# A hybrid decoder layer: v and gate products as a pinned three-step pipeline, norms by one-column sums and a way through DRAM, rotations swapped by ScalarE, merges with six open products

## The chip, the cores and the metric

The kernel runs on one core of one Trainium2 chip. The metric is the device time of one execution in microseconds. The kernel before takes 2696.99 us, the median of 3 runs (2695.11 to 2697.38).

## The reference

One layer of a decoder trunk over 512 tokens with 2048 channels (D), everything in float32. From the normalized and modulated u a combined projection gives the columns of three token mixers, their SiLU gates z and three merge gates g:

```python
u = rms_norm(x, norm_w) * (1.0 + scale) + shift        # shift, scale, gate from silu(c) @ w_ada + b_ada
proj = einsum('bsd,de->bse', u, w_in)                  # 2048 x 23552
o_a = diff_attention(a_q, a_k, a_v)    # 8 heads, two softmaxes of width 64, rms_norm over the head's 128
o_b = retention(b_q, b_k, b_v)         # 8 heads of 64, rotated q and k, decay, rms_norm over the head's 128
o_c = dilated_mixture(c_q, c_k, c_v)   # 3 groups x 8 heads, windows with dilation 1, 4, 16
y_a = (o_a * silu(a_z)) @ w_proj_a     # likewise y_b and y_c: 1024 x 2048
merged = sigmoid(g_a) * y_a + sigmoid(g_b) * y_b + sigmoid(g_c) * y_c
out = rms_norm(x + gate * (merged @ w_out), final_norm_w)
```

`rms_norm(o)` is `o * rsqrt(mean(o*o) + 1e-6) * w`. The rotation of a pair (2i, 2i+1) in a head of B is `x * cos + rot * sin`, where rot swaps the two numbers of the pair and turns the sign of one.

## The kernel before, in words

**Precision.** Every large product is made of three float32r products. `mm3` (L151-154) takes the rounded operands (h) and what the rounding left (l) and adds h·h, h·l and l·h into one PSUM tile. So each weight tile is first split: ScalarE copies the loaded tile r to h, VectorE subtracts, l = r − h. Activations lie transposed: channels on partitions, the 512 tokens along the free axis (`uh`, `ul`, 16 tiles of 128x512). PSUM has two tiles named `pj` and six named `at`, each 128x512. Weights pass through `wr`, `wh`, `wl` with three buffers each (L124-128).

**Stages.** After the start (norm, modulation, u, and the columns of the C gate, nine of its sixteen tiles without the shift's part) come in this order:

- The *units* (L488-665). Nine products of u with 1024 columns of `w_in`, each by seven products of half-size blocks instead of eight (in Winograd's way): three groups of v for C, one of v for A, one for B, and four half gates of A and B. A unit is a list of jobs: P1, P2 and R3 with two steps each (a step is four row tiles of 128 by 512 columns, one load of 1 MB into `xr`), then eight steps in which `sum_prep` adds blocks of the weights (four additions, L583) and `sum_mul` feeds four products R6, R5, R7 and Q4. Each step splits its tile, `xh` by ScalarE (L552, L584) and `xl` by VectorE (L553, L585); `xr` has three buffers, `xh` and `xl` two. The token forms fh, fl (sums of blocks of u) are built by `form_build` in the first eight steps from u read back out of DRAM. When P1, P2, R3 or the sums are complete, `keep`, `p2_done` or `sum_done` combine them; `put` writes the result to DRAM, for gate units after a sigmoid on ScalarE (L636). Job i + 1 is prepared ahead of the products of job i (L655-661). The order of the units' early halves is set by hand (L646): the plain steps of unit 3, then those of unit 2.
- The *C heads* (eight passes): per head seven projections (`proj`, L156-170: 2048 channels by 128 columns, 48 products) with scores, softmax and values of the head before placed at the middle of a projection (`mid`). Each pass starts with `bias_step` (L810-816): GpSimd computes, for one of nine 128-column tiles of the C gate, what the shift adds (`gate_bias_load`, L674-687, four loads, `br` with one buffer); one pass later TensorE sums it over the partitions (`gate_bias_sum`, L689-692).
- The *C merge*: `gate_phase` (L695-742) with mode "first". For each of sixteen tiles of 128 output channels: eight mm3 over the mixer's channels (yh, yl), times the sigmoid of the gate, plus the partial sum of the mixers before. `gate_cols` loads the gate's tile into `gsg` (two buffers), the partial sum comes back through `gpr` (one buffer) and goes out to `part_dram`. Three tiles are started ahead with six of their eight mm3 (`y_start`), and after each of them one piece of the last head's remaining work (`left`) is placed; the rest are started and closed one by one. `aux` adds a part of the output gate (product of c with `w_ada`, L756-796) behind each tile.
- The *A heads* (L1046-1087): q, k, scores, softmax (`a_scores`), transposes (`a_turn`), values, then the norm: `rms_squares` (L979-988) squares the output in halves, adds the halves, splits the sum into h and l on 64 partitions each; `rms_gate` (L990-998) sums over the partitions and spreads the sum with one 128x512 product with ones, takes root and reciprocal of the whole 128x512 tile, multiplies by the weight, the norm and silu(z), and `put_y` splits the result into yh and yl. The pieces of head n stand in the middle of the projections of head n + 1.
- The *A merge* ("mid"), the *B heads* in four pairs (L1128-1169; `rotate`, L1099-1107, with q and k of two heads side by side; even and odd numbers of the pairs lie in separate groups of 32 partitions, so the swap is a shift by 32 partitions), and the *B merge* ("last"), whose sums mh, ml stay in SBUF for the last product with `w_out`.

**What sets the order.** Each engine runs its instructions in one order. The framework's planner sets it at build time: it plays the program with costs of its own and takes the first instruction, in the order of the program, that its model says is ready. `tc.keep_in_program_order(instr)`, which the kernel before doesn't use in the functions below, holds an instruction behind the one traced before it on the same engine. DMAs are issued in each issuing engine's order: loads of weights, gates and partial sums by SyncE (SP), partial sums out by ScalarE, units' results and broadcasts by GpSimd.

## Time and profile before

| | |
|---|---|
| median of 3 runs | 2696.99 us (2695.11 to 2697.38) |
| the profiled execution's own time | 2694.27 us |
| its span in the profile | 2692.5 us |
| TensorE (PE) busy | 2578.1 us, 96% |
| VectorE (DVE) busy | 1695.3 us, 63% |
| ScalarE (ACT) busy | 1034.6 us, 38% |
| GpSimd (POOL) busy | 268.9 us, 10% |
| HBM read and written | 405.56 and 40.44 MB |

The profile is one execution. Times are microseconds from the span's start. PE stands for TensorE's products, PEld for its weight loads, which overlap them; SPq, ACTq and POOLq are the queues through which these engines issue DMAs. L552 is line 552 of the kernel before. A row "PE at L152 <- ACT yh L218: 11.8, 3, 6.4" says that PE, ahead of line 152, waited 11.8 us in total for ScalarE's writing of yh in line 218, three times, 6.4 us at the longest. PEclk is the granted clock of TensorE, 1.00 being full. By stage the span divides at about 239 (units begin), 964 (C heads), 1662 (C merge), 1756 (A heads), 2066 (A merge), 2184 (B heads), 2414 (B merge) and 2520 us (last product).

### The profile page before, as it was taken

Reading aid. Unit: us, or ns where it says so; the run is one execution under the profiler, and the core shown is the slowest. Engines: PE = TensorE matmul, PEld = TensorE weight load, DVE = VectorE, ACT = ScalarE, POOL = GpSimd, SP = SyncE. Lnnn points to the kernel's source line nnn. Section 1 sums busy time; section 2 is a strip of 40 time slices with the busy share of each in tenths; the row PEclk is TensorE's granted clock in tenths of the full one; section 3 lists DMA queues with packets and bytes.
Section 4 is the critical chain, followed back from the end, with each engine's and each line's share of the span. In section 5 each row is a group of like instructions: output and inputs, shape, how many; then the busy total and the mean of one; then the engine's idle time right before and its main releaser. Section 6 shows DMA issues by size and latency. Waiting matters only on the chain.

```text
span 2692.5 us, 33258 instructions
## 1 busy us (share of the span) xinstructions
PE 2578.1 (96%) x13091; PEld 2188.5 (81%) x13091; DVE 1695.3 (63%) x2456; ACT 1034.6 (38%) x1388; POOL 268.9 (10%) x271
## 2 busy tenths in 40 slices
PE   6899999999999999899999999999999899998998
PEld 5677878789999988788888888788887677777888
DVE  7995887877787744334443444657766667776434
ACT  4234433333343433333333333246665134443222
POOL 3432000000000022132211220000000000000000
PEclk9999999999999999999999999999999899999999
DMA  9776666666656655334444444943232773325632
GB/s 347 247 275 239 231 212 219 219 220 209 212 196 204 208 145 137 94 106 126 113 118 108 112 125 128 286 126 87 86 94 84 231 236 90 106 82 176 219 102 102
DMA packets 413420, 448.17 MB, mean 166 GB/s; under 512 B 24696, under 2 KB 308042, under 8 KB 412112
## 3 DMA queue, kind: packets, MB, share of 16 engines
q1 hardware_dynamic: 383784, 395.61, 46.6%
q0 software_dynamic: 9760, 33.59, 4.0%
q10 hardware_dynamic: 19720, 16.86, 1.8%
q8 instruction: 102, 1.67, 0.3%
q14 instruction: 54, 0.44, 0.1%
HBM read 405.56 MB, written 40.44 MB: 166 GB/s over the span
## 4 chain that ended last, share of the span: by engine, by line
PE 78%; DVE 12%; DMA 5%; ACT 2%; issue 2%; POOL 0%; SPq 0%; DVEq 0%; ACTq 0%; POOLq 0%
PE pj L154 15%; PE pj L153 15%; PE pj L152 15%; PE at L154 10%; PE at L153 10%; PE at L152 10%; DVE acc L312 3%; DMA xr<-in_w_in_dram 2%; DVE xl L553 1%; DMA part<-gsg 1%; DVE rt L1105 1%; DVE rs L995 1%; DMA gpr<-part 1%; DVE wl L148 1%; ACT xh L552 1%
## 5 line engine op out<-in xcount | busy, mean ns | idle before, releaser
L154 PE MATMUL pj<-uh,wl 128*128 128x512 f32 x1552 | 610.2, 393 | 12.1 <-DVE wl L148 9.5
L152 PE MATMUL pj<-uh,wh 128*128 128x512 f32 x1552 | 614.1, 396 | 4.8 <-ACT wh L147 4.8
L153 PE MATMUL pj<-ul,wh 128*128 128x512 f32 x1552 | 608.5, 392 | 0.0
L148 DVE TENSOR_TENSOR wl<-wr,wh 128x1024 fp32r<-128x1024 f32 x226 | 282.4, 1251 | 368.0 <-ACT wh L147 349.2
L147 ACT CAST wh<-wr 128x1024 fp32r<-128x1024 f32 x228 | 239.0, 1050 | 540.3 <-PE pj L153 395.3
L154 PEld LDWEIGHTS pj<-uh,wl 128*128 128x128 f32 x1552 | 293.8, 189 | 76.3 <-DVE wl L148 11.9
L152 PEld LDWEIGHTS pj<-uh,wh 128*128 128x128 f32 x1552 | 294.1, 189 | 63.9 <-ACT wh L147 5.0
L153 PEld LDWEIGHTS pj<-ul,wh 128*128 128x128 f32 x1552 | 294.0, 189 | 58.6
L584 ACT CAST xh<-xr 128x2048 fp32r<-128x2048 f32 x72 | 137.6, 1912 | 235.8 <-PE at L154 104.1
L583 DVE TENSOR_TENSOR xr<-xr 128x512 f32<-128x512 f32 x288 | 197.3, 690 | 41.5 <-DMA xr<-in_w_in_dram 36.0
L585 DVE TENSOR_TENSOR xl<-xr,xh 128x2048 fp32r<-128x2048 f32 x72 | 164.7, 2289 | 43.3 <-ACT xh L584 43.1
L152 PE MATMUL at<-yh,wh 128*128 128x512 f32 x384 | 155.2, 405 | 18.4 <-ACT yh L218 11.8
L553 DVE TENSOR_TENSOR xl<-xr,xh 128x2048 fp32r<-128x2048 f32 x54 | 123.8, 2293 | 55.3 <-ACT xh L552 54.8
L154 PE MATMUL at<-yh,wl 128*128 128x512 f32 x384 | 154.5, 402 | 3.9 <-DVE wl L148 3.7
L153 PE MATMUL at<-yl,wh 128*128 128x512 f32 x384 | 153.9, 401 | 0.0
L552 ACT CAST xh<-xr 128x2048 fp32r<-128x2048 f32 x54 | 103.0, 1908 | 128.0 <-PE at L153 52.0
L152 PE MATMUL at<-fh,xh 128*128 128x256 f32 x384 | 108.7, 283 | 0.0
L153 PE MATMUL at<-fl,xh 128*128 128x256 f32 x384 | 108.7, 283 | 0.0
L154 PE MATMUL at<-fh,xl 128*128 128x256 f32 x384 | 108.7, 283 | 0.0
L152 PEld LDWEIGHTS at<-yh,wh 128*128 128x128 f32 x384 | 74.8, 195 | 36.0 <-ACT yh L218 13.0
L153 PE MATMUL at<-xl,fh 128*128 128x512 f32 x240 | 93.5, 390 | 1.1 <-DVE xl L553 1.1
L154 PE MATMUL at<-xh,fl 128*128 128x512 f32 x240 | 93.4, 389 | 0.0
(408 smaller groups left out, 5144.9 us busy)
## 6 DMA issues: line engine op xcount, KB each, us to landing
wr<-in_w_in_dram SPq DMA_DIRECT2D x196, 512.0 KB, 3.9
xr<-in_w_in_dram SPq DMA_DIRECT2D x144, 512.0 KB, 4.4
xr<-in_w_in_dram SPq DMA_DIRECT2D x54, 1024.0 KB, 5.6
wa<-in_w_ada_dram SPq DMA_DIRECT2D x20, 1024.0 KB, 9.8
gwa<-in_w_ada_dram SPq DMA_DIRECT2D x32, 512.0 KB, 5.7
wr<-in_w_out_dram SPq DMA_DIRECT2D x32, 512.0 KB, 3.8
wr<-in_w_in_dram SPq DMA_DIRECT2D x32, 448.0 KB, 6.7
wb<-in_w_ada_dram SPq DMA_DIRECT2D x12, 1024.0 KB, 8.8
```

Source lines behind the costliest of these rows:

```text
L147: act.copy(h, r)
L148: low.tensor_sub(l, r, h.bitcast(F32))
L152: nc.tensor.matmul(ps, lhsT=ah, rhs=bh, start=start, stop=False)
L153: nc.tensor.matmul(ps, lhsT=ah, rhs=bl, start=False, stop=False)
L154: nc.tensor.matmul(ps, lhsT=al, rhs=bh, start=False, stop=stop)
L312: dve.scalar_tensor_tensor(out=acc, in0=wa[:, j, :], scalar=sc[:, k:k + 1], in1=acc, op0=ALU.mult, op1=ALU.add)
L552: act.copy(h, r)
L553: dve.tensor_sub(l, r, h.bitcast(F32))
L583: dve.tensor_add(r[:, o, :], r[:, o, :], r[:, a, :])
L584: act.copy(h, r)
L585: dve.tensor_sub(l, r, h.bitcast(F32))
L995: dve.reciprocal(rs, rs)
```

## The change

1. *Units.* The products, copies and VectorE operations of the units are held in the order of the program. Loads are traced two jobs ahead (`pure_load`, `sum_load`), the split (`x_split`) one job ahead, the products follow: three steps. `form_build` stands ahead of them. `sum_done` is cut into `done_z`, `done_s`, `done_rest`, one of which is traced after each following job.
2. *Bias.* `br` has two buffers; one load more is started near the end of head 4; the sums of all open loads are made at the start of the next head.
3. *Merges.* `gate_phase` opens six tiles ahead ("last": four) with seven (six) mm3 each; the rows of the weights for the missing ones come in one tile of their own (`h7`, `l7`). The first two of the open products use `pj`. The pieces of the last head stand after the tiles named in `places`. Closing then goes up to two tiles per newly started tile. The output gate's parts are two per tile, over eight tiles.
4. *Norms* in A and B. The whole output is squared at once; four products with one column of ones sum it over the partitions into a 128x4 tile (token on partition); root and reciprocal are of this tile; it is written to a row of 512 numbers in DRAM and read back to all partitions. The multiplication with the weight and silu(z) is done meanwhile, the one with the norm (`rms_put`) in the middle of the projection after the one in whose middle the sums are made.
5. *Rotations.* ScalarE copies the four groups of 32 partitions to their swapped places, VectorE multiplies once by sin, which is loaded with its groups swapped. One of the two subtractions for k's low part becomes a copy by ScalarE.

The diff, cut to its core:

```diff
+    def pin(instr):
+        if pinned[0]:
+            tc.keep_in_program_order(instr)
...
+        pin(nc.tensor.matmul(ps, lhsT=ah, rhs=bh, start=start, stop=False))
...
+    def x_split(r):
+        h = wxp.tile([P, 4, 512], F32R, tag="xh", name="xh", bufs=2)
+        l = wxp.tile([P, 4, 512], F32R, tag="xl", name="xl", bufs=2)
+        pin(act.copy(h, r))
+        pin(dve.tensor_sub(l, r, h.bitcast(F32)))
+        return h, l
...
-        def pure_prep(k0, cc):
-            r, h, l = x_tiles()
+        def pure_load(k0, cc):
+            r = wxp.tile([P, 4, 512], F32, tag="xr", name="xr", bufs=3)
             nc.sync.dma_start(out=r, in_=w[k0:k0 + 512, cc:cc + 512].rearrange("(j p) c -> p j c", p=P))
-            act.copy(h, r)
-            dve.tensor_sub(l, r, h.bitcast(F32))
-            return h, l
+            return r
...
+        def sum_load(j):
+            r = wxp.tile([P, 4, 512], F32, tag="xr", name="xr", bufs=3)
...
             for o, a in ((0, 1), (1, 3), (3, 0), (2, 3)):
-                dve.tensor_add(r[:, o, :], r[:, o, :], r[:, a, :])
-            act.copy(h, r)
-            dve.tensor_sub(l, r, h.bitcast(F32))
-            return h, l
+                pin(dve.tensor_add(r[:, o, :], r[:, o, :], r[:, a, :]))
+            return r
...
+        def done_z():
+            z = st["z"] = evp.tile([P, 2, 512], F32, tag="z", name="z")
             for q in range(2):
+                pin(dve.tensor_sub(z[:, q, :], st["R6"][q], st["p1"][:, q, :]))
+        def done_s():
...
+                pin(dve.tensor_add(s[:, q, :], z[:, q, :], st["R5"][q]))
+            pin(dve.tensor_add(r3, r3, s))
             put(r3, 0, 512)
+        def done_rest():
...
+                pin(dve.tensor_add(z[:, q, :], z[:, q, :], st["R7"][q]))
+                pin(dve.tensor_add(s[:, q, :], s[:, q, :], st["R7"][q]))
             put(s, 1, 512)
             for q in range(2):
+                pin(dve.tensor_sub(z[:, q, :], st["Q4"][q], z[:, q, :]))
             put(z, 1, 0)
...
+    raws = [jobs[0][0](), jobs[1][0]()]
+    ready = x_split(raws.pop(0))
...
+    pinned[0] = True
+    later = []
     for i, (_, mul, done) in enumerate(jobs):
-        nxt = jobs[i + 1][0]() if i + 1 < len(jobs) else None
         if i < HJ:
             form_build(i)
+        if i + 2 < len(jobs):
+            raws.append(jobs[i + 2][0]())
+        nxt = x_split(raws.pop(0)) if raws else None
         mul(ready)
         ready = nxt
+        later += done
+        for _ in range(len(later) if len(done) == 1 else min(1, len(later))):
+            later.pop(0)()
+    pinned[0] = False
...
-        br = pool.tile([P, P], F32, tag="br", name="br", bufs=1)
+        br = pool.tile([P, P], F32, tag="br", name="br", bufs=2)
...
+        n_ahead, late, places = {"first": (6, 1, (0, 2)), "mid": (6, 1, (0, 1, 2, 4)), "last": (4, 2, (0, 1, 3))}[mode]
...
-        def y_start(db):
+        def y_start(db, nj):
             h, l = w_half(w_p[0], 0, db * P)
-            py = at()
-            for j in range(6):
-                mm3(py, h[:, j, :], l[:, j, :], yh[j], yl[j], j == 0, False)
-            return py, h, l
+            py = pj() if db < 2 else at()
+            for j in range(nj):
+                mm3(py, h[:, j, :], l[:, j, :], yh[j], yl[j], j == 0, j == 7)
+            return py
...
+        for db in range(n_ahead):
+            ahead[db] = y_start(db, 8 - late)
+            if db in places:
                 left.pop(0)()
+        r, h7, l7 = w_tiles([P, late, n_ahead * P])
+        nc.sync.dma_start(out=r, in_=w_p[0, 1024 - late * P:1024, 0:n_ahead * P].rearrange("(j p) c -> p j c", p=P))
+        act.copy(h7, r)
+        dve.tensor_sub(l7, r, h7.bitcast(F32))
         gate_cols(0)
...
+        def close(db):
             if db + 1 < KC:
                 gate_cols(db + 1)
+            py = ahead.pop(db)
+            if db < n_ahead:
+                cs = slice(db * P, (db + 1) * P)
+                for j in range(late):
+                    y = 8 - late + j
+                    mm3(py, h7[:, j, cs], l7[:, j, cs], yh[y], yl[y], False, y == 7)
...
+        close(0)
+        done = 1
+        for db in range(n_ahead, KC):
+            ahead[db] = y_start(db, 8)
+            for _ in range(2 if db - done > 1 else 1):
+                if done < db:
+                    close(done)
+                    done += 1
             if aux is not None:
+                aux(db - n_ahead)
+        close(KC - 1)
...
     def bias_step():
-        if bias_open:
-            gate_bias_sum(*bias_open.pop())
+        while bias_open:
+            gate_bias_sum(*bias_open.pop(0))
+        bias_more()
...
-        if hd == 1:
-            bias_step()
+        if hd == 4:
+            bias_more()
...
     def gate_aux(db):
-        for _ in range(2 if db == 0 else 1):
+        for _ in range(2):
             if gsum:
                 gate_sum()
-            if db < KC - 1:
+            if db < 8:
                 gate_part()
...
+    def rms_square(pool, o):
+        sq = pool.tile([P, S], F32, tag="sq", name="sq")
+        act.activation(out=sq, in_=o, func=AF.Square)
+        return sq
+
+    def rms_sums(pool, o, sq, wcol, sz):
         ps = at()
+        for i in range(NT):
+            nc.tensor.matmul(ps[:, i:i + 1], lhsT=sq[:, i * P:(i + 1) * P], rhs=ones[:, 0:1],
+                             start=i == 0, stop=i == NT - 1)
+        rt = pool.tile([P, NT], F32, tag="rt4", name="rt4", bufs=2)
+        act.activation(out=rt, in_=ps[:, 0:NT], func=AF.Sqrt, scale=1.0 / P, bias=eps)
+        dve.reciprocal(rt, rt)
+        row = dram.tile([1, S], F32, tag="row", name="row", bufs=4)
+        nc.scalar.dma_start(out=row.rearrange("o (i p) -> p (o i)", p=P), in_=rt)
+        rs = pool.tile([P, S], F32, tag="rs", name="rs", bufs=2)
+        nc.gpsimd.dma_start(out=rs, in_=row[0].partition_broadcast(P))
+        dve.scalar_tensor_tensor(out=sz, in0=o, scalar=wcol, in1=sz, op0=ALU.mult, op1=ALU.mult)
+        return rs
+
+    def rms_put(pool, rs, sz, slot):
+        dve.tensor_mul(sz, sz, rs)
+        put_y(pool, slot, sz)
...
+        put_before = left[3]
+        ps = proj(A_Q + hd * P, mid=first)
...
+    for to in range(0, P, 32):
+        nc.sync.dma_start(out=sin[to:to + 32, :], in_=k_sin[to ^ 32:(to ^ 32) + 32, :])
...
         for to in range(0, P, 32):
             at_ = to ^ 32
-            dve.tensor_mul(t2[to:to + 32, :], ps[at_:at_ + 32, :], sin[at_:at_ + 32, :])
+            act.copy(t2[to:to + 32, :], ps[at_:at_ + 32, :])
+        dve.tensor_mul(t1, ps, cos)
+        dve.tensor_mul(t2, t2, sin)
         dve.tensor_add(t1, t1, t2)
...
-            for part in (own, other):
-                dve.tensor_sub(kl[part, :], kf[own, :], kh[own, :].bitcast(F32))
+            dve.tensor_sub(kl[own, :], kf[own, :], kh[own, :].bitcast(F32))
+            act.copy(kl[other, :], kl[own, :].bitcast(F32))
...
+        def z_mid(a, before=left[2:], pr=pr, ks_=ks_, qs=qs, pts=pts, values=values):
+            if before[a] is not None:
+                before[a]()
+            b_scores(2 * pr + a, ks_[a], qs[a], pts[a])
+            if pr == 3 and a == 1:
+                values(0)
...
+        def second(values=values, sums=sums):
+            sums(0)
             values(1)
...
+        def third(put=put, sums=sums):
+            put(0)
+            sums(1)
...
+        left = [lambda f=values: f(0), second, third, lambda f=put: f(1)]
...
+    gate_phase(G_B, w_pb, "last", mh, ml, left=[second, lambda: sums(1), lambda: (put(0), put(1))],
+               then=merged_open)
```

123 lines of the change are left out of this document (42 added, 81 removed).

## The prediction

> **What bounds the kernel now.** The page comes first: TensorE is busy for 96% of the span and leads the chain of work that ended last. Time can come only out of TensorE's idle stretches, so I read next the table of windows cut by stage (us; busy and count of PE, PEld, DVE, ACT, POOL; granted clock; DMA share; GB/s), then the waits of PE, then the pieces of the chain around each wait.
>
> ```profile
> span 2692.5 us, 33258 instructions
> PE 2578.1 (96%) x13091; PEld 2188.5 (81%) x13091; DVE 1695.3 (63%) x2456; ACT 1034.6 (38%) x1388; POOL 268.9 (10%) x271
> 239.00:964.00 725.00, 710.57 (x4370) 638.49 (x4368) 564.30 (x566) 280.14 (x186) 25.37 (x35) 1.00 0.63 213
> 964.00:1662.00 698.00, 682.72 (x3255) 572.94 (x3256) 288.62 (x533) 244.51 (x390) 157.57 (x196) 0.99 0.44 117
> 1662.00:1756.00 94.00, 91.23 (x411) 74.95 (x410) 55.75 (x73) 28.86 (x36) 1.88 (x2) 0.98 0.84 262
> 1756.00:2066.00 310.00, 307.26 (x1439) 254.42 (x1439) 212.36 (x418) 187.25 (x319) 0.00 (x0) 1.00 0.32 94
> 2066.00:2184.00 118.00, 101.66 (x415) 80.22 (x414) 75.42 (x112) 30.59 (x46) 0.00 (x0) 0.93 0.70 223
> 2184.00:2414.00 230.00, 215.65 (x952) 175.41 (x951) 171.92 (x269) 102.97 (x184) 0.00 (x0) 0.98 0.38 111
> 2414.00:2520.00 106.00, 98.16 (x421) 79.97 (x420) 64.18 (x76) 33.66 (x43) 0.00 (x0) 0.95 0.58 187
> ```
>
> In order: the units (products of v and the gates), the C heads, the C merge, the A heads, the A merge, the B heads, the B merge. The stages before 239 and after 2520 are not edited. The idle of the edited stages, length minus busy PE, is 14.4, 15.3, 2.8, 2.7, 16.3, 14.4 and 7.8 us, 73.7 together. A clock below 1 costs at most its lack times the length: 3.6 (within the rounding), 7.0, 1.9, 1.6, 8.3, 4.6 and 5.3. No more can be won.
>
> ```profile
> PE at L152 <- ACT yh L218: 11.8, 3, 6.4
> PE at L691 <- POOL br L686: 10.5, 1, 10.5
> PE at L1116 <- ACT k0h L1144: 4.2, 1, 4.2
> PE at L1030 <- DVE e L1021: 3.7, 2, 1.8
> ```
> ```profile
> 1136.00:1152.00 16.00, 5.51 (x17) 4.20 (x16) 2.41 (x6) 3.87 (x8) 6.89 (x10) 0.68 0.24 69
> 2262.00:2318.00 56.00, 52.84 (x232) 42.60 (x231) 43.89 (x70) 27.02 (x49) 0.00 (x0) 0.97 0.33 94
> ```
>
> Each large wait has one owner: the bias column br, the last norms (yh), the keys' split (k0h), a softmax's e. The clock falls behind each: in 16 us around the br wait its mean is 0.68. If it is 0.5 where it is low, it was low for 0.64 × 16 = 10 us, of which 5.5 held work, so some 2.7 us of work were lost; I count 2 us of clock for every wait above 3 us. The Trainium skill ("TensorE: Matmul & The Clock Gate", Part 1) says that the clock drops to half after an idle window of about 3.4 us and needs as long to rise; the row's 0.68 agrees, and by its 3.4 us the price of one wait would be 1.7 instead of 2.
>
> From the pieces of the chain (start, length): one half-size product (128x256) of a gate unit, a run of 15 full ones, and two pieces of the norm chain that follows it:
>
> ```profile
> 714.88 0.12 PE at L152
> ...
> 2084.84 0.23 PE at L152
> ...
> 2088.01 0.23 PE at L154
> ...
> 2089.23 3.36 DVE rs L995
> ...
> 2093.47 0.70 DVE rs L997
> ```
>
> 14 steps in 3.17 us: 0.226 us each. A step of a v unit is 24 of them, 5.45 us; of a gate unit 48 products of 128x256 at 0.12, 5.76 us.
>
> **The change part by part.** Durations come from one profiled execution of 2694.27 us (span 2692.5), which lies 2.7 under the median of the runs shown, 2696.99. I sum against 2694.3 and add 2.7 at the end.
>
> *1. Pinned units.* Now a planner orders these instructions; pinned, TensorE, ScalarE's and VectorE's run as written.
>
> ```profile
> L516 DVE TENSOR_TENSOR d<-xr 128x256 f32<-128x256 f32 x8 | 3.3, 421 | 0.6 <-DMA graw<-raw 0.6
> L520 ACT CAST fh<-d 128x1024 fp32r<-128x1024 f32 x8 | 8.4, 1050 | 8.8 <-DVE d L519 8.8
> L552 ACT CAST xh<-xr 128x2048 fp32r<-128x2048 f32 x54 | 103.0, 1908 | 128.0 <-PE at L153 52.0 <-PE at L154 34.1 <-DVE s L606 17.6
> L553 DVE TENSOR_TENSOR xl<-xr,xh 128x2048 fp32r<-128x2048 f32 x54 | 123.8, 2293 | 55.3 <-ACT xh L552 54.8
> L636 ACT ACTIVATE z<-z 128x1024 f32<-128x1024 f32 x4 | 4.2, 1060 | 0.6
> L565 ACT COPY p<-pj 128x512 f32<-128x512 f32 x18 | 10.6, 587 | 36.3 <-PE pj L154 35.8
> ```
>
> In the steady state it holds: xh and xl have two buffers, so the split for the next step waits for the end of the step before; copy 1.91 + subtraction 2.29 = 4.2 fits in 5.45. VectorE's four adds of 128x512 (0.70 each, as L997) and one subtraction, 2.8 + 2.29 = 5.09, fit too, just.
>
> The first eight steps: form_build now stands ahead of the split on both engines, and each engine needs the other: 4 × 0.42 + 1.05 + 1.91 + 2.29 = 6.9, with three hand-overs of 0.05, 7.05, in place of 5.45. That is 1.6 × 8 = 12.8, and about 3.7 once, as the raw copies occupy ScalarE when it starts: 16.
>
> Between sums and plain steps: done_s, done_rest and keep are traced in the steps after the sum, ahead of later copies on ScalarE, and in the gates each put is a sigmoid of 1.06. Counted from the end E of the last sum step: copy 1.9, subtraction 4.3, done_s (an 128x1024 addition counts as two: 4 × 0.70 less 0.2) 6.9, sigmoid 8.0, next copy 9.9, subtraction 12.3, done_rest's six operations and last sigmoid 17.6, two keep copies at 0.59 (18.8), copy 20.7, subtraction 23. The step that needs it would start at E + 17.75. So 4.5 to 5 us is lost, and 0.5 in the step before, at each of three gate boundaries: 15, with 2 us of clock each 21. The sigmoids themselves carry no pin; I take two thirds, 14, ends 0 and 21. v units have no sigmoid and pass. p2_done's two operations (1.4) and the sums' four adds ahead of one subtraction cost 0.9 in each of seven units: 6. The early unit's return adds some 5.5.
>
> Together 16 + 14 + 6 + 5.5 = 41.5, in place of what the stage loses now and which pinning replaces: its 14.4 idle and up to 4 of clock. 41.5 − 18.4 = **+23**. Ends: −14 if every stall goes and nothing new appears; +42 if each boundary costs its 7 and each second form step also waits 3 us for its rows.
>
> *2. Bias.* br gets a second buffer and one load more, in head 4: the wait of 10.5 and its clock of 2 to 2.7 go: −13 (0 if the loads stay late). POOL has the room, busy 157.6 of 698, and the loads that were held back by the one buffer start a head earlier.
>
> *3. Merges with six open products.*
>
> ```profile
> SPq L714 <- DMA part<-gsg: 49.7, 14, 5.0
> SPq L710 <- DMA part<-gsg: 47.3, 12, 7.7
> part<-gsg ACTq DMA_DIRECT2D x32, 256.0 KB, 4.5
> gpr<-part SPq DMA_DIRECT2D x32, 256.0 KB, 4.1
> ```
>
> The three extra open products need 3 × 21 × 0.227 = 14 us that now come before the first closing; no product is added, one weight split a merge is, behind 28 us of products. Closings are then two to a step until caught up. One closing holds a gsg buffer for load (as gpr's) 4.1, two operations 1.4 and write 4.5 = 10 us; with two buffers that is 5 us each, and gpr, one buffer, gives 4.1 + 1.4 = 5.5 where it is used (A and B); a full product takes 5.45: it keeps pace and no better. SP already stands 97 us behind the part writes, with weights queued after it. C merge: six products 28.6, two closings from buffers filled early, 14 × 5: 99 us in place of 94; TensorE has the next heads' projections for the 5: 0 (−3 to +13, a clock drop and 1 us more for every second closing). A merge: the wait for e (3.7 + 2 of clock) goes, as no reciprocal of 3.36 stands before it; the last yh wait, 6.4 + 2, is covered by products 3 to 5 (14 us against about 13, below). 14.1 less half for closings pressed together: −8 (−18 to +5).
>
> *4. Norms by columns and DRAM; 5. rotations.*
>
> ```profile
> L995 DVE RECIPROCAL rs<-rs 128x512 f32<-128x512 f32 x16 | 53.6, 3350 | 8.7 <-ACT rs L994 8.6
> L323 PE MATMUL pj<-ones,acc 128*128 128x1 f32 x96 | 12.8, 247 | 5.6 <-DVE acc L312 5.6
> L1105 DVE TENSOR_TENSOR rt<-pj,sin 32x512 f32<-32x512 f32 x32 | 22.0, 687 | 0.5
> bounce<-st ACTq DMA_DIRECT2D x8, 4.0 KB, 11.2
> bounce<-wt ACTq DMA_DIRECT2D x8, 4.0 KB, 1.9
> wtb<-bounce POOLq DMA_DIRECT2D x8, 512.0 KB, 5.9
> ```
>
> Per head VectorE loses the reciprocal 3.35 (four columns remain, 0.15 at most), one addition and one subtraction (0.69 with 64 rows too, the time goes by columns: L1105): 4.7. TensorE has four products in place of one: 4 × 0.25 busy at most, 4 × 0.11 if they overlap as half-size ones do: +0.2 to +0.8 a head, +4 for 16. The new way: the row's write scatters 512 pieces of 4 bytes. The nearest rows are the bounces, 1024 pieces in 11.2 and 256 in 1.9; by count 512 lies near 5, ends 1.9 and 11.2. Then the broadcast, at most 5.9, multiplication 0.69, copy 0.6 (L565), subtraction 0.69: 13 (10 to 19). In the heads another projection lies between (48 × 0.227 = 10.9 and more), so it hides; in the B merge only products 2 and 3 do, 2 × 18 × 0.227 = 8.2, so 5 us are late, less the start of the next open product. ScalarE issues the row's write and waits for the small reciprocal first, at most 0.15 + 0.1; behind it stand the next head's copies. POOL, which issues the broadcast, does nothing else there (0.00 in the rows). Sin's load becomes four on SP, once. The Trainium skill ("DMA: Bandwidth & Descriptors", Specifications) wants pieces of at least 512 B for full rate; the 11.2 us row agrees that 4-byte pieces are slow, and by its fixed 2.0 us a DMA (Anatomy of one DMA) the round trip would be 4 us, the tail hidden and the time 2677.
>
> Rotation: four 0.687 multiplications become one; ScalarE gets four copies at about 0.6 (as L565): VectorE −2.1, ScalarE +2.4, twice a pair, and one of two key subtractions (0.69, twice a pair) becomes a copy. A pair in VectorE's table: 43.9 − 2 × 4.7 − 4.2 − 1.4 = 29 of 56; ScalarE 27.0 + 4.8 + 1.2 and two operations of 0.6 fewer a head, 30.6. Both have room. Stage idle 14.4 plus 4.6 of clock: I take 11 of the 19 (4 to 17), as products still wait for k (4.2), whose chain is no shorter: 4 × 0.6 + 2 × 0.69 = 3.8 against 6 × 0.69 = 4.1. The B merge's tail now has two norms with their reciprocals in series. Of its 7.8 idle and 5.3 of clock, 5 and 3 come back as the late row: −5 (−11 to +3, if the write takes 11.2). A heads: −1 (−3 to +4). The columns' +4 is inside these.
>
> Sum: +23 − 13 + 0 − 8 − 1 − 11 − 5 = −15. 2694.3 − 15 = 2679.3, plus 2.7: **2682**.
>
> **The rivals.**
>
> (a) Pinning is cheap: the chains of forms and gates overlap better than written, no planner's stall is left, and the stage gains 14 instead of losing 23: 2682 − 37 = 2645. For it: ScalarE is idle behind PE for 86 of 128 us at L552, so it has time. Against it: the 7.05 is a closed circle of two engines, which idle time doesn't shorten.
>
> (b) Slower: the closings' buffers decide in the merges. With c us a closing a merge lasts 28.6 + 14c; the C merge is longer than now from c = 4.7 on, the A merge (118 us) from 6.4. If the load waits in SP's queue behind weights that wait themselves, 2 us more a closing, c = 7: 127 us, +33 and +9; the next heads cover half, 21, and the A merge's 8 isn't won: 2682 + 21 + 8 = 2711. For it: SP's 97 us, up to 7.7 at once. Against it: the bytes are the same, and the gsg loads can be issued a closing ahead.
>
> (c) The norm's way through DRAM is the new wait: its write takes the upper 11.2 and delays the B merge by 6 more and each of three B pairs by 3: +15, 2697, no change.
>
> (d) The pin does nothing, as the planner's order is nearly this one: the stage stays as it is, 2682 − 23 = 2659. For it: the two-buffer splits force much of the order. Against it: the forms and gates are placed by the planner now in another order than written, as its 14.4 us of idle, a third of the written order's 41.5, tells.
>
> **How the numbers follow.** My forecast 0.4, with its own range 2664 to 2700; (a) 0.15; (b) 0.2; (c) 0.1; (d) 0.15. About 0.2% (5.4 us) is what a measurement of this kernel can tell from no change: below 2691.6 is faster. Of the forecast's 0.4, 0.27 lie there, 0.07 within and 0.06 above; (a) and (d) are faster; (b) slower, but for 0.01; (c) mostly the same, 0.06, else 0.01 faster and 0.03 slower. Faster 0.27 + 0.3 + 0.01 = 0.58, same 0.07 + 0.01 + 0.06 = 0.14, slower 0.28. The range takes in (a) and most of (b): 2645 to 2713.
>
> **What would show it.** Forms: PE waits of 1.5 us for xl in the first eight steps, mean PE share there near 0.8. Gate boundaries: two or three waits near 4.5 for xh or xl behind a sigmoid. Bias: no row for br. Merges: gsg or part first among SP's waits. Norms: a row's write near 5 us and one wait for yh near 4 in the B merge; no 3350 ns reciprocal. B pairs: VectorE near 29 us in a pair. I am wrong if the unit stage, now 725 us, gets shorter, or if a merge stretches by over 10 us.

## The result

The changed kernel takes 2788.29 us, the median of 4 runs (2786.17 to 2790.68), beside 2696.05 us (2690.72 to 2697.38) of the kernel before in the same session: 1.0346 times the time, 95% interval 1.0328 to 1.0364. It is 92 us slower; I had forecast 15 us faster, with a range that ended at 2713.

### The profile page after: what moved, and what is told of

It reads as the page before. It is cut to its first block, busy times and chain, and to the rows that moved or that the text cites. A ratio compares the mean times of both kernels' runs of the same rounds, so it can differ in the third digit from the quotient of the medians.

```text
span 2788.9 us, 33579 instructions
## 1 busy us (share of the span) xinstructions
PE 2616.5 (94%) x13203; PEld 2223.4 (80%) x13203; DVE 1615.4 (58%) x2395; ACT 1020.4 (37%) x1392; POOL 277.1 (10%) x287
## 5 line engine op out<-in xcount | busy, mean ns | idle before, releaser
L161 PE MATMUL at<-yh,wl 128*128 128x512 f32 x336 | 135.7, 404 | 8.4 <-DVE wl L148 8.4
L159 PE MATMUL at<-yh,wh 128*128 128x512 f32 x336 | 135.7, 404 | 5.4 <-ACT wh L147 4.4
L160 PE MATMUL at<-yl,wh 128*128 128x512 f32 x336 | 134.3, 400 | 0.0
L159 PE MATMUL at<-xh,fh 128*128 128x512 f32 x240 | 95.2, 397 | 5.8 <-DVE s L614 5.8
L1047 DVE TENSOR_TENSOR sz<-sz,rs 128x512 f32<-128x512 f32 x16 | 11.1, 692 | 149.4 <-DMA rs<-row 149.4
L161 PE MATMUL at<-wh,ml 128*128 128x512 f32 (+1 forms) x256 | 92.8, 362 | 0.0
```

The source lines that it names most:

```text
L159: pin(nc.tensor.matmul(ps, lhsT=ah, rhs=bh, start=start, stop=False))
L160: pin(nc.tensor.matmul(ps, lhsT=ah, rhs=bl, start=False, stop=False))
L161: pin(nc.tensor.matmul(ps, lhsT=al, rhs=bh, start=False, stop=stop))
L1047: dve.tensor_mul(sz, sz, rs)
```

## The profile after

The first lines of its page. TensorE is still the engine that is busy most, but the span grew by 96.4 us, of which only 38 are busy time. The clock is lower in the table below, and there are 112 more products; n_row16, a run below with the same number of products, is busy 2588.1 us, 10 more than before.

```profile
span 2788.9 us, 33579 instructions
PE 2616.5 (94%) x13203; PEld 2223.4 (80%) x13203; DVE 1615.4 (58%) x2395; ACT 1020.4 (37%) x1392; POOL 277.1 (10%) x287
```

The table of windows of the changed kernel, cut at the same places of the work as the one of before (columns as there: length; busy and count of PE, PEld, DVE, ACT, POOL; granted clock; DMA share; GB/s):

```profile
239.00:994.00 755.00, 724.72 (x4370) 648.26 (x4369) 574.57 (x568) 281.13 (x187) 25.33 (x35) 0.98 0.60 205
994.00:1681.00 687.00, 681.73 (x3258) 572.32 (x3259) 289.58 (x533) 244.26 (x390) 157.41 (x196) 1.00 0.45 120
1681.00:1777.00 96.00, 91.01 (x410) 74.91 (x409) 56.47 (x71) 27.43 (x34) 1.85 (x2) 0.98 0.80 243
1777.00:2123.00 346.00, 321.47 (x1483) 267.79 (x1482) 185.54 (x416) 169.56 (x308) 3.30 (x6) 0.96 0.34 93
2123.00:2251.00 128.00, 105.22 (x417) 82.49 (x416) 68.64 (x100) 26.54 (x38) 1.07 (x2) 0.89 0.66 202
2251.00:2493.00 242.00, 212.53 (x961) 176.74 (x960) 115.63 (x212) 110.16 (x200) 3.23 (x6) 0.93 0.41 111
2493.00:2616.00 123.00, 109.31 (x474) 88.91 (x474) 64.58 (x87) 36.49 (x49) 1.07 (x2) 0.94 0.58 178
```

Against the seven lengths of before (725, 698, 94, 310, 118, 230, 106 us): units +30, C heads −11, C merge +2, A heads **+36**, A merge +10, B heads +12, B merge +17. The A heads had hardly any idle time before (2.7 us) and have 24.5 now, with the clock down to 0.96. The stages with a norm of the new kind all grew, while VectorE's busy time fell in the A heads (212.4 to 185.5) and in the B heads (171.9 to 115.6): the saved work is there, the time isn't.

The largest waits of TensorE in the changed kernel are new or have grown; the second fence has, from VectorE's list of waits, the one that the timelines below connect with them.

```profile
PE at L1177 <- ACT k0h L1205: 27.9, 4, 8.7
PE pj L159 <- ACT yh L225: 24.8, 4, 10.3
PE at L1080 <- DVE e L1071: 23.5, 6, 5.0
```
```profile
DVE sz L1047 <- DMA rs<-row: 149.4, 15, 15.8
```

VectorE stands 149.4 us, 15 times, ahead of line 1047, the multiplication in `rms_put` by the norm read back from DRAM. The list of DMA issues gives both halves of the round trip (the last number is the median from issue to landing):

```profile
row<-rt ACTq DMA_DIRECT2D x16, 2.0 KB, 9.9
rs<-row POOLq DMA_DIRECT2D x16, 256.0 KB, 4.5
```

The timeline of one A head (start, length, engine, line; in brackets the idle time before), VectorE's rows first, then those of ScalarE's queue, GpSimd and TensorE, shows what hangs on it:

```profile
1898.86 0.62 DVE L1071 SCALAR_TENSOR_TENSOR e<-e,st 128x384 f32<-128x384 f32 x1
1899.39 0.15 DVE L1069 TENSOR_TENSOR st<-st,nlam 128x1 f32<-128x1 f32 x1
1907.14 0.69 DVE L1047 TENSOR_TENSOR sz<-sz,rs 128x512 f32<-128x512 f32 x1 [7.60 <-DMA rs<-row]
1907.75 0.48 DVE L1070 TENSOR_SCALAR e<-e,st 128x512 f32<-128x512 f32 x1
1908.27 0.75 DVE L1071 SCALAR_TENSOR_TENSOR e<-e,st 128x512 f32<-128x512 f32 x1
...
1893.43 0.38 ACTq L1040 DMA_DIRECT2D row<-rt  x1
...
1902.64 0.54 POOL L1042 DMA_DIRECT2D rs<-row  x1 [44.23 <-DMA row<-rt]
...
1904.50 0.82 PE L1080 MATMUL at<-ident,e 128*128 128x128 f32 x6
1909.08 0.74 PE L1080 MATMUL at<-ident,e 128*128 128x128 f32 x4 [3.76 <-DVE e L1071]
```

VectorE has done three of the four row blocks of the softmax at 1899.5. The next instruction in its order is line 1047 of the head before; its data land at 1907.1. The last block of the softmax (lines 1070 and 1071) stands behind it, ready all the time; TensorE's transposes wait 3.76 us for that block; the mean clock of the stage is 0.96. In three of the four B pairs the multiplication stands ahead of the rotation (L1165) of the keys, and TensorE waits for k0h; in the merges it holds up yh itself. The rows of the second pair and of the B merge:

```profile
2341.55 0.69 DVE L1047 TENSOR_TENSOR sz<-sz,rs 128x512 f32<-128x512 f32 x1 [12.82 <-DMA rs<-row]
...
2343.30 0.69 DVE L1165 TENSOR_TENSOR rf<-pj,cos 128x512 f32<-128x512 f32 x1
...
2347.13 1.43 PE L1177 MATMUL at<-q,k0h 128*128 128x512 f32 x4 [8.43 <-ACT k0h L1205]
...
2527.58 0.69 DVE L1047 TENSOR_TENSOR sz<-sz,rs 128x512 f32<-128x512 f32 x1 [15.80 <-DMA rs<-row]
```

## The experiments

Below, medians of the runs in one session with the kernel before (2691.8 to 2693.3 in these sessions), and the ratio to it with its 95% interval. Numbers in its second column are the parts of the change. The second table gives the stages, from 239 us on, by the start times of products in the profiles: the last with xh or xl; the last score of C; the first and the last score of A; the first and the last product of the first value block of a B pair; the first product with the merged sums. Each row is one profiled execution, and stages that an edit doesn't touch differ too: the C merge by some 4 us between p12 and p125, whose edit lies in the B heads.

| run | what it has | median us | ratio, interval |
|---|---|---|---|
| p2_bias | 2 | 2679.91 | 0.9959, 0.9946 to 0.9971 |
| p12_units_bias | 1, 2 | 2713.64 | 1.0081, 1.0063 to 1.0098 |
| p125_units_bias_rot | 1, 2, 5 | 2698.54 | 1.0024, 1.0013 to 1.0035 |
| p1235_all_but_norms | 1, 2, 3, 5 | 2682.71 | 0.9971, 0.9960 to 0.9982 |
| n_row16 | all, row in 128 pieces | 2687.65 | 0.9980, 0.9971 to 0.9990 |
| n_pe_spread | all, no row | 2700.84 | 1.0029, 1.0017 to 1.0041 |
| n_late | all, A's put later | 2779.67 | 1.0333, 1.0311 to 1.0356 |
| n_pin_late | all, put later and held | 2747.01 | 1.0209, 1.0192 to 1.0226 |
| u_forms | 1, 2, forms later | 2700.07 | 1.0027, 1.0016 to 1.0038 |
| u_no_sigmoid | 1, 2, no sigmoid | 2691.15 | 0.9997, 0.9985 to 1.0009 |
| b_pe_no_units | 2 to 5, no row | 2670.07 | 0.9916, 0.9901 to 0.9931 |
| b_mix | 2, 3, 5, norm in B's pairs | 2656.17 | 0.9870, 0.9854 to 0.9886 |
| p25_bias_rot | 2, 5 | 2669.32 | 0.9915, 0.9896 to 0.9933 |
| p23_bias_merges | 2, 3 | 2668.27 | 0.9911, 0.9896 to 0.9925 |
| p235_no_units_no_norms | 2, 3, 5 | 2653.28 | 0.9855, 0.9839 to 0.9872 |

| stage, us | units | C heads | C merge | A heads | A merge | B pairs | B merge |
|---|---|---|---|---|---|---|---|
| before | 724.7 | 688.7 | 130.4 | 277.8 | 181.0 | 168.2 | 98.9 |
| after | 754.6 | 677.0 | 133.5 | 313.9 | 191.0 | 179.3 | 116.7 |
| p2_bias | 725.6 | 675.2 | 129.3 | 277.8 | 180.1 | 165.5 | 98.8 |
| p12 | 756.2 | 675.6 | 130.3 | 277.8 | 179.5 | 165.5 | 98.8 |
| p125 | 758.2 | 676.2 | 134.2 | 277.7 | 182.9 | 155.7 | 98.7 |
| p1235 | 756.1 | 675.8 | 134.9 | 277.8 | 165.8 | 155.7 | 91.9 |
| n_row16 | 756.7 | 676.4 | 134.7 | 277.6 | 171.9 | 145.9 | 100.0 |
| n_late | 756.3 | 676.2 | 135.5 | 309.4 | 183.6 | 176.8 | 113.2 |
| n_pin_late | 756.6 | 676.3 | 136.8 | 277.6 | 187.5 | 176.4 | 116.5 |
| u_forms | 746.0 | 676.3 | 130.6 | 277.7 | 179.7 | 165.6 | 98.7 |
| u_no_sigmoid | 737.2 | 674.2 | 130.4 | 277.7 | 180.9 | 165.0 | 98.7 |
| b_mix | 728.8 | 676.0 | 133.9 | 277.7 | 172.0 | 154.6 | 92.1 |
| p25 | 729.2 | 676.1 | 132.9 | 277.8 | 178.5 | 155.6 | 98.1 |
| p23 | 726.0 | 675.1 | 136.2 | 278.0 | 173.4 | 164.9 | 91.9 |
| p235 | 725.0 | 675.1 | 134.8 | 277.9 | 166.6 | 155.5 | 92.1 |

### One part after the other

**p2_bias**: of the diff, only

```diff
-        br = pool.tile([P, P], F32, tag="br", name="br", bufs=1)
+        br = pool.tile([P, P], F32, tag="br", name="br", bufs=2)
...
-        if bias_open:
-            gate_bias_sum(*bias_open.pop())
+        while bias_open:
+            gate_bias_sum(*bias_open.pop(0))
+        bias_more()
...
-        if hd == 1:
-            bias_step()
+        if hd == 4:
+            bias_more()
```

> The kernel before with part 2 alone (br with two buffers, one load more in head 4, sums drained at the start of the next head). My working prices it at 13 us: the wait of 10.5 for br and 2 to 2.7 of low clock; the time should be 2681 to 2686. If the loads stayed late, 2696 as before. In the changed kernel the C heads took 11.6 us less between the first product of the last units and the last scores, so 2684 is likeliest.

Measured: 2679.91, 12 us less; no wait for br is left and the C heads are 13.5 us shorter.

**p12_units_bias**: the same, and all edits of the units (`pin`, `x_split`, the three steps, `done_z`, `done_s`, `done_rest`).

> Parts 1 and 2 alone (units pinned, bias with two buffers). In the changed kernel the unit stage ends 30 us later than before. If pinning itself is the cause this kernel is 30 us (27 to 33) above the one with the bias alone, near 2714. If instead the later stages pushed it (they come after the units, so they cannot by order, only by memory layout) it would equal the one with the bias alone, 2684.

Measured: 2713.64, 33.7 us more than with the bias alone; the unit stage is 31 us longer, the later stages are as before. So the edits of the units themselves are the cause, and not a later stage. The pins and the new order of the steps come together in this run; none separates them.

**p125_units_bias_rot**: the same, and

```diff
-            dve.tensor_mul(t2[to:to + 32, :], ps[at_:at_ + 32, :], sin[at_:at_ + 32, :])
+            act.copy(t2[to:to + 32, :], ps[at_:at_ + 32, :])
...
+        dve.tensor_mul(t2, t2, sin)
...
+            act.copy(kl[other, :], kl[own, :].bitcast(F32))
```

> Parts 1, 2 and 5 (rotations swapped by ScalarE, one key subtraction turned into a copy), with the norms and the merges of before. If the rotation relieves VectorE in the B heads as the prediction had it, this is 3 to 8 us below the kernel with parts 1 and 2 (near 2708). Rival: the wait for the keys (k0h, 27.9 us in the changed kernel) is the rotation's doing, since its copies on ScalarE stand in the chain of the keys; then it is 10 to 25 us above (2724 to 2739).

Measured: 2698.54, 15 us less, more than the 3 to 8 expected. The rival falls: copies on ScalarE don't lengthen the way to the keys. The profiled execution of this run is its slowest one (2707.85) and that of p12 its fastest (2708.40), so the sizes are taken up again below, with one part each.

**p1235_all_but_norms**: the same, and the merges' edits, with three pieces of the last head in place of four:

```diff
-        n_ahead, late, places = {"first": (6, 1, (0, 2)), "mid": (6, 1, (0, 1, 2, 4)), "last": (4, 2, (0, 1, 3))}[mode]
+        n_ahead, late, places = {"first": (6, 1, (0, 2)), "mid": (6, 1, (0, 1, 2)), "last": (4, 2, (0, 1, 2))}[mode]
```

> All parts but the norms, which stay as before (one product with ones, reciprocal of 128x512, no DRAM). Theory: the norms' way through DRAM causes the loss in the A and B heads and at the end of the A and B merges, 36 + 10 + 11 + 18 us less what was there before; without it this kernel is 70 to 85 us below the changed one, 2703 to 2718. Rival: the six open products cause part of it (buffers gsg and gpr, SP's order); then this kernel is 10 to 25 us above the kernel with parts 1, 2 and 5.

Measured: 2682.71. Set beside the changed kernel by their ratios, 1.0346 − 0.9971 = 0.0375 of some 2693: the norms alone cost 101 us, more than the 70 to 85 expected, since merges and rotations win more than I knew. The rival falls: beside p125 the medians are 16 us lower, so the merges win time.

**p25_bias_rot and p23_bias_merges**: the rotations, or the merges, on the bias alone (the same edits).

> Bias and rotations (parts 2 and 5), the rest as before. Between the kernels with parts 1, 2 and with 1, 2, 5 the medians fell by 15 us but the profiles by 0.5. If the rotations are worth the medians' 15, this is 2663 to 2668 against 2680 for the bias alone; if they are worth what the stages of the profiles show, 10 in the B pairs less 4 and 3 in the two merges before them, 2675 to 2679.

> Bias and merges (parts 2 and 3), the rest as before. The stages of the profiles give the merges 17 us in the A merge and 7 in the B merge, less 4 in the C merge: 2656 to 2664 if all of it stands; 2664 to 2668 if the medians' difference of 16 is right; 2676 or more if the merges' buffers cost what they win, as my rival (b) had it.

Measured: 2669.32, rotations −10.6, between the two values named; 2668.27, merges −11.6, just above the second of the three ranges expected. Both together, p235, win 26.6 against the bias alone, 4 more than the two added; that lies within the intervals of the ratios, so no surplus is shown.

### The norms

**n_row16**: the same 2 KB written in the tile's own order, so that each partition's four numbers form one piece:

```diff
-        nc.scalar.dma_start(out=row.rearrange("o (i p) -> p (o i)", p=P), in_=rt)
+        nc.scalar.dma_start(out=row.rearrange("o (p i) -> p (o i)", i=NT), in_=rt)
...
-        dve.tensor_mul(sz, sz, rs)
+        szv = sz.rearrange("q (i p) -> q i p", p=P)
+        dve.tensor_mul(szv, szv, rs.rearrange("q (p i) -> q i p", i=NT))
```

> The changed kernel, but the row of the norm is written in the order of the tile, 128 pieces of 16 bytes instead of 512 of 4; the multiplication reads it back in that order. Theory: the write takes 9.9 us (median of 16) because of its pieces, and VectorE, whose order is fixed, stands 149.4 us in 15 waits for the broadcast behind it. With 128 pieces the write should take 2 us (1.9 in the row of 256 pieces), the waits fall by some 8 us each to 30 to 50 us in total, and the time by 50 to 90 us to 2695 to 2738. Rival: the way through two DMA queues itself costs it, whatever the pieces; then the write still takes 6 us or more and the time falls by less than 25 us.

Measured: 2687.65, about 100 us less than the changed kernel (ratios 1.0346 and 0.9980), more than the 50 to 90 expected. Its DMA issues and VectorE's waits:

```profile
row<-rt ACTq DMA_DIRECT2D x16, 2.0 KB, 1.4
rs<-row POOLq DMA_DIRECT2D x16, 256.0 KB, 3.6
```
```profile
DVE sz L1048 <- DMA rs<-row: 26.6, 14, 4.2
```

The write takes 1.4 us in place of 9.9, for the same bytes from the same tile through the same queue. The A heads are back at 277.6 us, the B pairs at 145.9. The form of the write, 512 pieces of 4 bytes, is the cause of the loss; the way through two queues as such isn't. The number of the pieces and their size change together in this run.

**n_late**: in A, the multiplication one projection later in the program.

```diff
-        ps = proj(A_Q + hd * P, mid=first)
+        ps = proj(A_Q + hd * P, mid=left[0])
...
-        ps = proj(A_K + hd * P, mid=left[1])
+        ps = proj(A_K + hd * P, mid=second)
```

where `second` calls `put_before` and then `left[1]`.

> The changed kernel with the norm's multiplication of the A heads placed one projection (10.9 us) later, in the middle of the next head's keys instead of its queries; B as changed. Theory, in two halves: if the place in the program decides where VectorE stands, the six waits of the A heads (46.4 us of VectorE, 23.5 us of TensorE for e, and the low clock) go, 30 to 38 us less, near 2752. If the planner, which reckons with a shorter round trip, sets the place and its model had the data ready before the old place already, the order moves with the program too and the gain is the same; if it was the queues or the DMA itself that hold up the heads, the time stays at 2788.

Measured: 2779.67, 9 us less by the medians of two sessions, but no clear change by the ratios (1.0333 and 1.0346, with overlapping intervals); the A heads are 4.5 shorter. The 30 to 38 us that I expected are missed. The timeline of VectorE in this run tells why:

```profile
1901.32 0.15 DVE L1069 TENSOR_TENSOR st<-st,nlam 128x1 f32<-128x1 f32 x1
1908.88 0.69 DVE L1047 TENSOR_TENSOR sz<-sz,rs 128x512 f32<-128x512 f32 x1 [7.41 <-DMA rs<-row]
1909.49 0.48 DVE L1070 TENSOR_SCALAR e<-e,st 128x512 f32<-128x512 f32 x1
```

The multiplication still stands ahead of the last block of the softmax, in the same place as in the changed kernel, though the program has it one projection, some 11 us, later. Here the place in the program doesn't decide where VectorE does it; the planner does.

**n_pin_late**: the same, and the multiplication held in the program's order.

```diff
-        dve.tensor_mul(sz, sz, rs)
+        tc.keep_in_program_order(dve.tensor_mul(sz, sz, rs))
```

> As the run n_late (the norm's multiplication of the A heads one projection later in the program), and the multiplication is held in the order of the program on VectorE; the row is still written in 512 pieces of 4 bytes. In n_late VectorE did the multiplication at the same place as in the changed kernel, ahead of the last pieces of the softmax, whatever its place in the program. Theory: the loss of the A heads is the planner's early place times the long write; held at its late place the wait is gone, the A heads fall from 309 to 314 back to 278 us, and the time by 30 to 40 us to 2740 to 2755 (the B heads' multiplications are held too, at their place of before in the program, so they may win up to 20 more). Rival: the queue behind the write (ScalarE's or GpSimd's) holds up the heads; then the A heads stay above 300 us.

Measured: 2747.01, as expected. The A heads take 277.6 us (expected 278), with the row still written in 9.3 us. VectorE's wait in the stretch of the A heads, 1809 to 2086 us, and TensorE's busy time there (window row, columns as above):

```profile
DVE sz L1047 <- DMA rs<-row: 30.0, 6, 7.5
```
```profile
1809.00:2086.00 277.00, 276.44 (x1342) 233.04 (x1342) 167.44 (x376) 151.15 (x276) 3.30 (x6) 1.00 0.33 92
```

VectorE still waits 30 us, and TensorE loses 0.6: at this later place nothing that TensorE needs stands behind the wait. So in the A heads it takes both, the long write and the early place; either cure brings the stage back. In the B pairs and the merges the place was held but not later, and nothing clear was won there (B pairs 176.4 beside 176.8 in n_late, the two merges 3 to 4 us longer).

**n_pe_spread**: no DRAM; the reciprocals are spread by TensorE.

```diff
-        row = dram.tile([1, S], F32, tag="row", name="row", bufs=4)
-        nc.scalar.dma_start(out=row.rearrange("o (i p) -> p (o i)", p=P), in_=rt)
-        rs = pool.tile([P, S], F32, tag="rs", name="rs", bufs=2)
-        nc.gpsimd.dma_start(out=rs, in_=row[0].partition_broadcast(P))
...
+            nc.tensor.matmul(rs[:, i * P:(i + 1) * P], lhsT=rt[:, i:i + 1].broadcast_to([P, P]), rhs=ident,
+                             start=i == 0, stop=i == NT - 1)
```

> The changed kernel without the row in DRAM: four more products (the column of reciprocals as weights, repeated, times the identity) spread them over the partitions in PSUM, where the multiplication reads them. No DMA is left in the norm. Theory: with the round trip gone its whole cost goes, and the saved reciprocals of 3.35 us remain as a gain over the kernel with the norms of before (2683): 2660 to 2680. Rival: the one-column sums and the later placement cost something by themselves; then it stays above 2690.

Measured: 2700.84, a miss: the round trip is gone, but it is 13 us slower than with the fast row. TensorE is busy 13.6 us longer than in n_row16 (2601.7 against 2588.1), and TensorE is what bounds the kernel: its A heads take 283.2 us, n_row16's 277.6. The row of the new products (the profile counts each of the 64 as two):

```profile
L1045 PE MATMUL at<-ident,rt 128*128 128x128 f32 x128 | 16.7, 274 | 0.0
```

13.6 / 16 is 0.85 us a head, against a row through DRAM, which puts no product on TensorE.

**b_pe_no_units**: the same, with the units of before.

> The changed kernel with the units of before and the norm spread by TensorE (no DRAM row): parts 2, 3, 5 and the one-column sums. By the steps measured so far (units +34, norms +103) it should be 34 us below the kernel that only spreads by TensorE, 2628 to 2648, and faster than both the kernel before and the changed one.

Measured: 2670.07, 31 us below n_pe_spread, as the units cost, but 22 us above what I had expected, since the expectation was made before n_pe_spread had shown the price of spreading by TensorE.

### The units

**u_forms** (on parts 1 and 2): `form_build` is cut before its copy; the second half is traced behind the next split.

```diff
         nxt = x_split(raws.pop(0)) if raws else None
+        if 1 <= i <= HJ:
+            form_split(i - 1)
         mul(ready)
```

> Parts 1 and 2 (2713.6 in its run), with each form's copy and second subtraction traced one step later, behind the next split. Theory of the closed circle (four subtractions, copy of the form, copy and subtraction of the split, 7.05 us in a step of 5.45): with the form's copy behind the split the circle is open, VectorE has 5.2 us of work in a step of 5.45, and the first steps lose 8 to 14 us less: 2699 to 2706. Rival: the first steps wait for the rows out of DRAM or for the buffers xr; then it stays within 4 us of 2713.

Measured: 2700.07, 13.6 us less by the medians, 9 to 10 by the profiled executions; 8 to 14 were expected. Rows of the windows over the first steps, of parts 1 and 2, and of this run (TensorE busy 53.9 and 60.0 of 67 us):

```profile
243.00:310.00 67.00, 53.89 (x207) 41.19 (x206) 46.70 (x55) 28.73 (x22) 2.19 (x3) 0.92 0.63 221
```
```profile
243.00:310.00 67.00, 60.04 (x245) 47.35 (x245) 53.96 (x63) 31.84 (x25) 2.19 (x3) 0.95 0.70 251
```

That bears out the circle of two engines; by the rival, rows or buffers, the time would have stayed within 4 us of 2713.

**u_no_sigmoid** (on parts 1 and 2): the gates of A and B are stored without their sigmoid.

```diff
-            act.activation(out=t, in_=t, func=AF.Sigmoid)
```

> Parts 1 and 2 with the sigmoid of the stored gates (A and B) left out, so the gates are stored raw; nothing else changes. Theory: at the three boundaries between gate units 4.5 us and the low clock after it come from sigmoids that stand ahead of the split's copy on ScalarE in the fixed order; without them the boundaries lose 1 us at most and the time falls by 12 to 18 us to 2696 to 2702. Rival: VectorE's nine operations of the closing sums alone hold the split up; then it falls by less than 6 us.

Measured: 2691.15, 22.5 us less by the medians, 19 in the unit stage, above the 12 to 18 expected. The run also takes the sigmoids' own time off ScalarE, so it doesn't price their place in the order alone. In the timeline of ScalarE of the changed kernel the order at such a boundary can be read:

```profile
739.46 1.06 ACT L647 ACTIVATE r<-r 128x1024 f32<-128x1024 f32 x1 [4.81 <-DVE r L615]
740.42 1.89 ACT L507 CAST xh<-xr 128x2048 fp32r<-128x2048 f32 x1
747.06 1.06 ACT L647 ACTIVATE s<-s 128x1024 f32<-128x1024 f32 x1 [4.75 <-DVE s L622]
748.26 1.06 ACT L647 ACTIVATE z<-z 128x1024 f32<-128x1024 f32 x1
749.22 1.06 ACT L572 COPY p<-pj 128x512 f32<-128x512 f32 x2
750.17 3.71 ACT L507 CAST xh<-xr 128x2048 fp32r<-128x2048 f32 x2
```

Between the copies of 740.4 and 750.2 ScalarE waits 4.75 us for `done_rest`'s additions, does two sigmoids and two keep copies, and only then the split that TensorE needs.

### What the rest is worth

**b_mix** and **p235_no_units_no_norms**: parts 2, 3, 5 with the units of before; b_mix has besides the one-column norm, with the fast row, in the first three pairs of B.

> A version meant to be faster: units and A norms of before, bias, merges and rotations as changed, and in B the one-column norm only in the first three pairs, with its row written in 128 pieces of 16 bytes; the last pair, whose norm ends in the B merge, has the norm of before. From the stage lengths of the runs so far: the kernel with all but norms 2683, units of before -32, B pairs -10: 2636 to 2648.

> Bias, merges and rotations (parts 2, 3, 5) with the units and the norms of before: what the change is worth without its two costly parts. From all but norms, 2682.7, less the 33.7 of the pinned units: 2645 to 2653, the fastest so far if the one-column norm of the mixed version (2656) wins nothing.

Measured: 2656.17, a miss by 8 us, and 2653.28, at the upper edge of what was expected. Their intervals overlap: the one-column norm, even with a fast row, wins nothing here. B pairs and B merge together take 246.7 us in b_mix, 245.9 in n_row16 and 247.6 in p1235 with the norm of before. In n_row16 the B pairs alone are 10 us shorter than in p1235, but its B merge is 8 us longer and its A merge 6; why b_mix, with the new norm in the same pairs, has them no shorter isn't settled. p235 is the fastest kernel found, 0.9855 of before.

## Why the prediction was wrong

**The step that failed is part 4**: "by count 512 lies near 5, ends 1.9 and 11.2 … 13 (10 to 19). In the heads another projection lies between …, so it hides." It fails in three places.

- *The size.* The write was priced near 5 by the number of pieces, between two rows that differ in the size of the pieces too, 4 and 16 bytes. It took 9.9 us. Among the four writes on record, twice as many pieces of one size cost 1.3 us more (4 bytes: 9.9 and 11.2) and 0.5 more (16 bytes: 1.4 and 1.9), while between the sizes lies a factor of 6 to 7; so the size weighs more, though no two runs differ in it alone.
- *The overlap.* Even 13 us don't fit into the 10.9 of a projection; "and more" had no row behind it.
- *The order.* I took the place in the program for the place in VectorE's order. n_late shows that the planner sets it: in the timeline VectorE stands at the multiplication 6 us after the row's issue (1899.5 and 1893.4), and the row lands 13.7 after it. What stands behind the waiting instruction I worked out for ScalarE and GpSimd ("behind it stand the next head's copies"), not for VectorE, where the new wait was.

The wait's term was 0 in the heads and 5 in the tail; the norms measured 101 us, of which the fast row brings back about 100. My rival (c) had the new wait and the upper end of the write, with 15 us for it, but it looked at B alone and not at what stands behind the wait on VectorE; 15 of 16 heads have it. The 4 us for the round trip in the sentence on the Trainium skill ("DMA: Bandwidth & Descriptors", Anatomy of one DMA) come from a figure that the page gives for transfers issued by GpSimd; the row's write is issued by ScalarE, and the two halves took 9.9 and 4.5 us, with pieces of 16 bytes 1.4 and 3.6.

Of the prediction's own signs of being wrong one came: the B merge stretched by 17 us. That p1235, the kernel without part 4, takes 2682.71, nearly the 2682 forecast for the whole, is luck: there the units cost more than forecast, and merges and rotations win more.

**The units**: forecast +23, measured +33.7 by the medians, 31 by the stage. The circle of the forms (16 expected) gave 13.6 back when opened, 10 in the stage. The gate boundaries were worked out at 21 and entered at 14, "the sigmoids themselves carry no pin"; without sigmoids 22.5 came back, 19 in the stage. In the timeline an instruction without a pin of its own, the sigmoid of line 647, does stand ahead of a pinned one traced after it. But the three boundaries themselves lose less than 21: in 16 us around each (from 744, 829 and 918 us) TensorE does 86, 87 and 80 half-size products, where without a wait it does 129 (before, from 714 us); at 0.12 us each that is some 16 us. So the sum without the discount, 48.5 less 18.4 = 30, fits the stage, but not term by term. The early unit's return, 5.5 in the sum, fits one wait of 5.8 us for the closing sums (s), near 360 us, that the changed kernel and these runs have. Rivals (a) and (d) fall.

**The bias**: −13 forecast, −12 measured.

**The merges**: C 0, A −8 and the B merge's share forecast; −11.6 measured on the bias alone (C merge +7, A merge −7, B merge −7 by the stages) and −16 on p125 (+1, −17, −7). The 14.1 less half gave 7, not 8. Rival (b) falls: it had the C merge 33 us longer.

**Norms and rotations in the B heads**: −11 for both. The rotations alone measured −10.6 (B pairs −10), the one-column norm with a fast row 0 or a little worse (b_mix beside p235, n_row16 beside p1235). So of VectorE's saved 4.7 us a head nothing arrives in the kernel's time; TensorE's idle time in the B heads hung on the rotation. In n_row16 TensorE is busy 10 us longer than in p1235 (2588.1 and 2578.4), where the four products were entered with 4.

**The clock**: the 24.5 us of idle time in the A heads and 0.04 × 346 = 13.8 us of low clock together, less the 2.7 and up to 1.6 of before, are some 34 of the 36 us that the stage grew by; some 2 us for each of six waits, as the prediction counted.

The measured parts: +34 for the units, −12 for the bias, −27 for merges and rotations, +101 for the norms, +96 together, beside 92 by the medians. They were measured on different bases and in several sessions, so the 4 us between the sums say nothing.

## What to carry to other kernels

A wait is priced at the engine whose order it stands in: list what is behind it there, in the order the engine really has, which the trace shows and the program's text doesn't; where a framework plans the order, an early place can turn a hidden transfer into a stall, and holding one instruction can cure it. Price a scattered write by the size of its pieces as well as their number, and lay the small tile's own order out in DRAM, so that the reading engine does the reordering. An order fixed by hand needs its circles summed in full, over every engine, with no discount that has no row behind it.

## What the runs showed of the hardware

- 2 KB from a tile of 128x4 to DRAM took 9.9 us (9.4 to 10.9) in 512 pieces of 4 bytes and 1.4 us in 128 of 16 bytes. The two bounces of before fit: 1024 of 4 bytes 11.2, 256 of 16 bytes 1.9. The Trainium skill ("DMA: Bandwidth & Descriptors", Specifications) names 512 B as the least size for full rate; here both sizes lie far below it, and the two writes of 2 KB differ by a factor of 7.
- VectorE's multiplication that reads one operand with a step of 16 bytes took 1.07 us, the plain one 0.69:

```profile
L1048 DVE TENSOR_TENSOR sz<-sz,rs 128x512 f32<-128x512 f32 x16 | 17.1, 1071 | 26.7 <-DMA rs<-row 26.6
```

- A matmul takes a column repeated by a step of zero as its weights (n_pe_spread), at an estimated 0.21 us each in f32 (13.6 us of busy time over 64 of them), about what a full 128x512 product in f32r takes (0.226).
